# A streaming encoder step on one core: half of the norming, the weights' sums and the GLU's operands move to other places of the program

## The chip, the cores and the metric

The kernel runs on one core of a Trainium2 chip. The core has five engines with queues of their own: TensorE (PE in the profile, PEld for its weight loads), VectorE (DVE), ScalarE (ACT), GpSimd (POOL) and SyncE (SP), which issues the transfers. The metric is the device time of one execution, in microseconds (us). A time given for a kernel is the median of several runs; a profile is one further execution, with a time of its own.

## The reference

One step of a one-layer hybrid encoder over 2048 prompt tokens and 64 tokens of a decode sequence (`D_MODEL` 1024), all in float32. Cut to what matters:

```python
mod = jax.nn.silu(c) @ w_ada + b_ada
shift, scale, gate = jnp.split(mod, 3, axis=-1)
h = _rmsnorm(x, norm_g) * (1.0 + scale[:, None, :]) + shift[:, None, :]
proj = h @ w_in                                   # 1024 x 3080
u, z_s, q, k, v, z_a, f_logit = jnp.split(proj, IN_SPLITS, axis=-1)   # 5 x 512, 512, 8
# S5: 32 groups of 16 channels, 64 complex states each, scan over time
y_ssm = jax.nn.gelu(y_ssm)
y_ssm = y_ssm * jax.nn.sigmoid(y_ssm @ w_glu + b_glu)       # 512 x 512
y_ssm = y_ssm * jax.nn.silu(z_s)
# FoX: 8 heads of 64, q and k normed, logits plus the running sum of log-forget
logf = jax.nn.log_sigmoid(f_logit + b_f)
o = _fox_attend(q, cum_q, pos_q, k, v, cum_k, pos_k)
y_att = o * jax.nn.silu(z_a)
y = x + gate[:, None, :] * (jnp.concatenate([y_ssm, y_att], axis=-1) @ w_out)
```

## The kernel before

A float32 product is made of three products of rounded parts: `mm3` (L145) splits both factors into a high and a low part and issues high by high, low by high and high by low. Each operand of a large product therefore has to be split first: a cast for the high part (L310 on ScalarE, L308 on VectorE) and a subtraction for the low one (L314 on VectorE, L196 on GpSimd).

The stages follow each other on TensorE:

1. **Norm** (class `InProj`). The 16 tiles of 128 prompt tokens and the decode tile form four groups g = 0 to 3. `load` fetches tiles of x (L473 squares, L475 scales them); `norm` turns them by TensorE (L148), applies the adaLN scale and shift (L500, ScalarE) and splits the result h (L308, L314). The scale and shift come from class `Ada`, whose six `chunk`s each read 2 MB of `w_ada` (L402); chunks 4 and 5 make the gate, which is needed only at the end. The parts of h of groups 0 and 2 share one place in SBUF, and so do those of 1 and 3: `put` stores groups 0 and 1 in DRAM, and `get` brings them back.
2. **In-projection**. `line` walks a list of stretches (kind, first column, row, groups, rate, what to do after a group). For each product (24 matmuls: 8 k steps by 3) it issues the product, fetches and splits the next stretch's weights (`fetch`, `part`), evicts the result (`channels` L582 and L572, `natural` L624), and advances a generator `side` by so many steps as the rate says. u of all four groups comes first, since the S5 needs all of it; then k, v, q and z of groups (2, 3); then the same of groups (0, 1).
3. **The side**. What `side` yields step by step is all the work that lies beside the projection: the S5's parameters, its 16 sets of groups (`s5.sets`), its final state, the log-forget sums (`logf`), the attention's `bias`, and `Out.operands`: eight times, four blocks of `w_out` are read, four of their sums are made (L1629, L1631 on VectorE, L196 on GpSimd), split, and stored in DRAM for the Strassen-like output product.
4. **GLU** (class `Glu`), run inside `Attn.glu` together with the maxima of the attention's logits: 16 blocks of 24 matmuls each.
5. **Attention** with the output's weights prepared beside it, and then the **output product**.

The order of the work: TensorE's instructions keep the order in which they are written out while `e.PE.strict` is set, and are otherwise ordered, as on the other engines, by a scheduler that works from a model of the costs; `tc.high_priority()` puts what is inside it ahead, and `tc.keep_in_program_order` pins an instruction. The products use three PSUM banks in turn (`low_132`, `low_136`, `low_140` in the order), the turning of x two others (`low_124`, `low_128`). Every transfer is issued by SyncE in order, so one that waits holds those behind it.

In the kernel before, the first half of u's columns is written out for groups 0 and 1 unstrictly, together with the second half of them; then chunks 4 and 5, the masks, and the norm of groups 2 and 3 are written out, and only then does the strict line begin. The functions, with the line numbers that the profile uses:

## Time and profile before

| what | value |
|---|---|
| median of 3 runs (1470.35 to 1474.24) | 1474.21 us |
| the profiled execution's own time | 1473.12 us |
| its span, first to last instruction | 1471.1 us |
| TensorE busy | 1329.3 us, 90% |
| VectorE busy | 976.3 us, 66% |
| ScalarE, GpSimd busy | 607.5 us, 493.0 us |
| mean granted clock of TensorE | 0.956 |

A row of the timeline reads: start, duration, engine, line, operation, what it writes and reads, and in brackets how long the engine stood idle before it and what ended the idle time. A row of the table by windows reads: the window, its length, then busy time and number of instructions of each engine, the granted clock, the share of the transfer engines and the rate of transfers. Stages can be found in the timeline by TensorE's rows: the projection's products write `low`, those of the GLU write `glu`, the logits write `twin`.

### The profile page before, as it was taken

Reading aid. Unit: us, or ns where it says so; the run is one execution under the profiler, and the core shown is the slowest. Engines: PE = TensorE matmul, PEld = TensorE weight load, DVE = VectorE, ACT = ScalarE, POOL = GpSimd, SP = SyncE. Lnnn points to the kernel's source line nnn. Section 1 sums busy time; section 2 is a strip of 40 time slices with the busy share of each in tenths; the row PEclk is TensorE's granted clock in tenths of the full one; section 3 lists DMA queues with packets and bytes.
Section 4 is the critical chain, followed back from the end, with each engine's and each line's share of the span. In section 5 each row is a group of like instructions: output and inputs, shape, how many; then the busy total and the mean of one; then the engine's idle time right before and its main releaser. Section 6 shows DMA issues by size and latency. Waiting matters only on the chain.

```text
span 1471.1 us, 25856 instructions
## 1 busy us (share of the span) xinstructions
PE 1329.3 (90%) x9160; PEld 1040.8 (71%) x9160; DVE 976.3 (66%) x2404; ACT 607.5 (41%) x1640; POOL 493.0 (34%) x444
## 2 busy tenths in 40 slices
PE   5888999999999799998953989999999999879998
PEld 2874988999889699996843875555555554358887
DVE  2637977787675577553532787788688787346775
ACT  3745134455443354443312434545535545522221
POOL 1101254355222343240122311432423425824443
PEclk9997999999999899999986989999999999989999
DMA  9856323333436534343676852324122111586452
GB/s 341 306 202 178 94 78 92 104 97 95 118 107 203 192 103 128 102 125 113 216 246 200 249 166 56 98 61 138 47 73 66 37 46 44 143 278 221 154 170 86
DMA packets 249474, 204.91 MB, mean 139 GB/s; under 512 B 91296, under 2 KB 217340, under 8 KB 248321
## 3 DMA queue, kind: packets, MB, share of 16 engines
q1 hardware_dynamic: 249344, 203.27, 45.0%
q8 instruction: 72, 1.18, 0.3%
q14 instruction: 58, 0.47, 0.1%
HBM read 137.68 MB, written 65.53 MB: 138 GB/s over the span
## 4 chain that ended last, share of the span: by engine, by line
PE 67%; DVE 10%; DMA 9%; SPq 4%; issue 4%; ACT 3%; POOL 2%; DVEq 0%; ACTq 0%; POOLq 0%
PE low L145 30%; PE bank L145 12%; PE twin L145 12%; PE last L145 9%; DMA x<-in_x_prompt_dram 3%; PE glu L145 3%; DVE pb L1361 2%; PE bank L148 2%; SPq L402 1%; DMA b<-in_w_out_dram 1%; DVE acc L1438 1%; DMA wst<-in_w_in_dram 1%; DMA ost<-in_w_out_dram 1%; SPq L1625 1%; POOL olb L196 1%
## 5 line engine op out<-in xcount | busy, mean ns | idle before, releaser
L145 PE MATMUL low<-whi,h 128*128 128x256 f32 (+1 forms) x1584 | 297.1, 286 | 14.4 <-DVE th L582 10.1
L145 PE MATMUL low<-h,whi 128*128 128x256 f32 (+2 forms) x1152 | 275.4, 331 | 6.2 <-ACT th L572 5.8
L145 PEld LDWEIGHTS low<-whi,h 128*128 128x128 f32 x1584 | 249.4, 191 | 17.0 <-DVE th L582 10.8
L1361 DVE CUSTOM_DVE_ANT_0 pb<-twin,cb 128x512 bf16<-128x512 f32 (+3 forms) x328 | 200.0, 610 | 60.9 <-PE twin L145 51.1
L145 PE MATMUL low<-wlo,h 128*128 128x256 f32 (+1 forms) x816 | 230.2, 285 | 4.8 <-DVE wlo L314 4.7
L145 PEld LDWEIGHTS low<-h,whi 128*128 128x128 f32 x1152 | 197.2, 193 | 24.7 <-ACT th L572 6.8
L345 ACT ACTIVATE p<-twin 128x1024 f32<-128x1024 f32 (+3 forms) x180 | 149.8, 840 | 119.4 <-PE twin L145 110.6
L145 PE MATMUL low<-h,wlo 128*128 128x256 f32 (+2 forms) x576 | 188.9, 329 | 2.2 <-DVE wlo L314 2.2
L145 PEld LDWEIGHTS low<-wlo,h 128*128 128x128 f32 x816 | 155.4, 190 | 7.3 <-DVE wlo L314 6.8
L145 PE MATMUL bank<-p,vt 128*64 128x512 f32 (+3 forms) x704 | 141.5, 524 | 0.0
L145 PE MATMUL twin<-qs,ks 64*128 64x512 f32 (+3 forms) x1056 | 134.0, 359 | 0.0
L145 PEld LDWEIGHTS low<-h,wlo 128*128 128x128 f32 x576 | 111.3, 193 | 11.4 <-DVE wlo L314 2.6
L1438 DVE TENSOR_TENSOR acc<-acc,p 128x1024 f32<-128x1024 f32 (+4 forms) x90 | 90.7, 1008 | 29.2 <-ACT p L345 26.6
L320 POOL TENSOR_TENSOR qss<-qss,mhalf 128x4 f32<-128x4 f32 (+1 forms) x68 | 73.6, 1084 | 102.1 <-DVE qss L319 99.5
L314 DVE TENSOR_TENSOR wlo<-wst,whi 128x512 fp32r<-128x512 f32 (+1 forms) x96 | 68.4, 723 | 53.5 <-ACT whi L310 53.3
L145 PEld LDWEIGHTS twin<-qs,ks 64*128 64x128 f32 x1056 | 94.6, 190 | 11.0
L145 PE MATMUL twin<-sm,kb 64*128 64x512 f32 (+3 forms) x360 | 77.6, 426 | 21.0 <-DVE pm L1361 14.3
L145 PEld LDWEIGHTS bank<-p,vt 128*64 128x64 f32 x704 | 45.1, 140 | 63.8 <-issue 56.0
L310 ACT CAST whi<-wst 128x512 fp32r<-128x512 f32 (+1 forms) x96 | 58.0, 625 | 64.4 <-DMA wst<-in_w_in_dram 48.9
L196 POOL TENSOR_TENSOR x<-x,ot 128x512 f32<-128x512 f32 (+1 forms) x34 | 52.8, 1557 | 88.7 <-DVE ot L1739 70.9
L620 ACT ACTIVATE ev<-low 128x64 f32<-128x64 f32 x256 | 53.6, 224 | 67.7 <-PE low L145 29.2
L145 PEld LDWEIGHTS twin<-sm,kb 64*128 64x128 f32 x360 | 34.3, 186 | 61.1 <-DVE pm L1361 32.7
(434 smaller groups left out, 2621.2 us busy)
## 6 DMA issues: line engine op xcount, KB each, us to landing
wst<-in_w_in_dram SPq DMA_DIRECT2D x48, 512.0 KB
x<-in_x_prompt_dram SPq DMA_DIRECT2D x32, 512.0 KB
h<-h SPq DMA_DIRECT2D x16, 1024.0 KB
wada<-in_w_ada_dram SPq DMA_DIRECT2D x12, 1024.0 KB
cb<-cb_d SPq DMA_DIRECT2D x20, 512.0 KB
out_dram<-ev SPq DMA_DIRECT2D x64, 128.0 KB
out_dram<-x SPq DMA_DIRECT2D x32, 256.0 KB
z_d<-th SPq DMA_DIRECT2D x24, 256.0 KB
```

What stands on the lines that cost most here:

```text
L145: return self.keep(self.pe.matmul(*a, **kw))
L148: return self.keep(self.pe.transpose(*a, **kw))
L196: PL.tensor_tensor(out, x, y, op=op)
L310: i = S.copy(hi, x)
L314: V.tensor_tensor(lo, x, hi, op=ALU.subtract)
L320: PL.tensor_tensor(out, out, bc(mhalf[:out.shape[0]], list(out.shape)), op=ALU.pow)
L345: i = S.activation(out, x, func, **kw)
L402: x = nc.sync.dma_start(w[:, 4 * k2:4 * k2 + 4], e.w_ada[512 * k2:512 * k2 + 512, n * 512:n * 512 + 512] .rearrange("(k p) c -> p k c", p=P))
L620: S.activation(tv[:, h], pv[:, h], AF.Square, accum_out=ss[:r, h:h + 1])
L1361: V.tensor_tensor_reduce(b[:, :n], ps[:, h, :n], cb[:, h, :n], 1.0, NEG, ALU.add, ALU.max, accum_out=self.pm[:, t, h, pi:pi + 1])
L1438: (PL if j else V).tensor_tensor(y[:rows, :, c0:nq], x[:rows, :, c0:nq], p[:rows, :, :n], op=ALU.add)
L1625: e.tc.keep_in_program_order(e.nc.sync.dma_start(b, self.block(i // 2, i % 2, k)[:, ns]))
```

## The change

Seven edits:

1. The **norm of groups 2 and 3** becomes a generator that yields after each pair of k tiles. A new generator `second` loads x of these groups, starts the transfers of adaLN's chunks 4 and 5, scales, norms group 2, finishes the chunks, norms group 3 and starts the S5's setup. It is the first part of the side. The line now begins with u's first product and takes u in four stretches: the first half of the columns for groups 0 and 1, the second half for 0, 1 and 2, the first for 2 and 3, the second for 3.
2. The side's steps are counted in fractions (`share`), so that a rate of 1.5 gives z 12 steps in a stretch where it gave 8 or 10 by whole numbers.
3. Evictions and the splits of the next weights are written inside `high_priority`, the first half of an eviction stands ahead of `after(g)`, the first split comes one product later (`at == 3`), and 256-wide u products are evicted into the ring "ev" with four buffers instead of "th" with two.
4. **Out.operands** is taken one step at a time at every ninth of the S5's sets' steps.
5. **Glu.start** becomes a generator at the end of the side: the transfer of `w_glu` is issued first, its low parts are made on VectorE, one k tile at a step; the first two parts of y are split there too.
6. Six empty steps instead of three after `logf`'s read.
7. In the attention's **last tile** the last two blocks of p are not added up on VectorE; they go as further matmuls into `sums`. Five steps of the output's weights come ahead of the last sums.

The diff, cut to its core:

```diff
@@ InProj.norm
+    def norm(self, g, steps=False):
...
+            if not steps:
+                if (g, i0) not in self.normed:
+                    self.load(g, i0)
+                self.scale(g, i0)
             xs = self.normed.pop((g, i0))
...
                 if s:
                     V.tensor_copy(hi[:, k:k + 2, c0 + w:c0 + 2 * w], lo[:, k:k + 2, c0:c0 + w])
+                yield
@@ InProj.channels
-        x = self.ev.tile([P, 512], F32, tag="th", name="th")
+        if kind == "u" and n == 256:
+            x = self.ev.tile([P, 256], F32, tag="ev", name="ue", bufs=4)
+        else:
+            x = self.ev.tile([P, 512], F32, tag="th", name="th")
@@ InProj.line
-                if nw and at == 2:
-                    self.part(nw)
-                if nw and not cur:
-                    while len(nw.hi) < KT:
+                with self.e.tc.high_priority():
+                    if nw and at == 3:
                         self.part(nw)
+                    if nw and not cur:
+                        while len(nw.hi) < KT:
+                            self.part(nw)
+                    next(b, None)
                 if after and (not cur or cur[1] != g):
                     after(g)
-                next(b, None)
-                for _ in range(int(size * rate)):
+                share += size * (rate[g] if isinstance(rate, dict) else rate)
+                while share >= 1:
+                    share -= 1
                     next(side, None)
-                for _ in b:
-                    pass
+                with self.e.tc.high_priority():
+                    for _ in b:
+                        pass
@@ InProj.logf
-        yield
-        yield
-        yield
+        for _ in range(6):
+            yield
@@ Attn
-        glu.start()
...
-        if acc[j] is None:
+        if tile.last and i >= tile.nb - 2:
+            tile.rest.append((p, rows, c0, n))
+        elif acc[j] is None:
...
+        ops += [(pt[64 * h:64 * h + 64, c0:nq], e.ones[:rows, :64], p[:rows, h, :m])
+                for p, rows, c0, m in tile.rest for h in (1, 0)]
...
+        for _ in range(5):
+            next(weights)
         self.sums(pend[0])
@@ Glu.start
+        st = []
+        for k in range(0, 4, 2):
+            st.append(self.wk.tile([P, 2, SW], F32, tag="wgs", name="wgs"))
+            e.nc.sync.dma_start(st[-1], e.w_glu[P * k:P * k + 256].rearrange("(k p) c -> p k c", p=P))
         for b in range(2):
             self.load(b)
-        for k in range(0, 4, 2):
-            st = self.wk.tile([P, 2, SW], F32, tag="wgs", name="wgs")
-            e.nc.sync.dma_start(st, e.w_glu[P * k:P * k + 256].rearrange("(k p) c -> p k c", p=P))
-            e.split(st, self.wh[:, k:k + 2], self.wl[:, k:k + 2])
+        for _ in range(3):
+            yield
+        for k in range(4):
+            e.split(st[k // 2][:, k % 2], self.wh[:, k], self.wl[:, k], el=e.V, keep=not k)
+            yield
         for b in range(2, 4):
             self.load(b)
         self.gate(0)
         for b in range(2):
             self.part(b)
+            yield
@@ the program
-        ip.line([("u", 0, 0, (0, 1), 0, None), ("u", 256, 256, (0, 1), 0, None)], nothing, w)
-        for n in (4, 5):
-            ad.chunk(n)
         e.masks()
-        for g in (2, 3):
-            ip.norm(g)
...
+        def second():
+            ip.load(2, 0)
+            ip.load(2, 2)
+            yield
+            gates = [ad.steps(n) for n in (4, 5)]
...
+            for n, _ in enumerate(ip.norm(2, True)):
+                if n % 4 == 3:
+                    ip.load(3, n // 4 * 2)
+                yield
+            for x in gates:
+                for _ in x:
+                    pass
+                yield
...
         def rest():
+            yield from second()
             yield from s5_setup
-            yield from s5.sets()
+            ops = (x for i in range(8) for x in out.operands(*divmod(i, 2)))
+            for n, _ in enumerate(s5.sets()):
+                if n % 9 == 6:
+                    next(ops, None)
+                yield
...
             yield from made[0].bias(s5.ps)
-            for i in range(8):
-                yield from out.operands(*divmod(i, 2))
+            made.append(Glu(e))
+            yield from made[1].start()
...
-        ts = [("u", 0, 0, (2, 3), 3, None), ("u", 256, 256, (2, 3), 3, None)]
+        ts = [("u", 0, 0, (0, 1), 0, None), ("u", 256, 256, (0, 1, 2), {0: 1, 1: 2, 2: 2.5}, None),
+              ("u", 0, 0, (2, 3), {2: 2.5, 3: 4}, None), ("u", 256, 256, (3,), 4, None)]
```

How instructions move, at three places. First TensorE where the gate's chunks lie. `wada` are the weights of a chunk, `ms` its copied result, `ident,x` a turned tile of x, `h` the parts of a group (the number after it is the place), `prow` the S5's parameters. Before:

```order
L145 MATMUL low_144<-wada_1_246,cT_0_176 32x512 x4
L148 MATMUL low_128<-ident_0_82,x_0_145 128x64 x2
L148 MATMUL low_124<-ident_0_82,x_0_145 128x64 x2
L145 MATMUL bank_77<-ms_1_257,sel_0_181 32x512
L145 MATMUL bank_81<-ms_1_257,sel_0_181 32x512
L148 MATMUL low_144<-ident_0_82,prow_0_1191 128x32 x4
L145 MATMUL low_140<-h_0_0_307,whi_3_223 128x256
```

The same chunk in the changed kernel:

```order
L145 MATMUL low_136<-h_36864_0_297,whi_2_208 128x256
L145 MATMUL low_136<-h_0_0_296,wlo_2_209 128x256
L145 MATMUL low_144<-wada_0_216,cT_0_165 32x512 x8
L145 MATMUL bank_77<-ms_0_227,sel_0_170 32x512
L145 MATMUL bank_81<-ms_0_227,sel_0_170 32x512
L145 MATMUL low_144<-wada_1_235,cT_0_165 32x512 x8
L145 MATMUL bank_77<-ms_1_246,sel_0_170 32x512
L145 MATMUL bank_81<-ms_1_246,sel_0_170 32x512
L145 MATMUL low_140<-h_0_0_296,whi_4_630 128x256
```

Before, a block of turned tiles of groups 2 and 3, of both chunks and of the parameters stands between two products, with no product inside. Now both chunks stand together between two products of u, with a product of 24 matmuls right ahead and behind; the turned tiles of group 2 stand eight at a time between the products ahead of this place, and those of group 3 between the products after it.

Second, SyncE's transfers of the GLU's weights (`wgs`). `t` are the stored sums of `w_out`, `vt` and `vn` the attention's values, `gz` the gates, `yt` the S5's outputs, `lf` the log-forget values, `z_d<-th` an evicted z product. Before:

```order
L1638 DMA t_69<-pl_3_7573 128x256
L1563 DMA yt_5_8130<-ys_d 128x2x264
L1303 DMA vt_3_9142<-out_dram 128x4x128
L1303 DMA vt_4_9326<-out_dram 128x4x128
L1299 DMA vn_1_9605<-out_dram 64x128
L1550 DMA wgs_0_8047<-in_w_glu_dram 128x2x512
L1569 DMA gz_0_8059<-z_d 128x2x264
L1550 DMA wgs_1_8051<-in_w_glu_dram 128x2x512
```

In the changed kernel:

```order
L1602 DMA gz_0_7884<-z_d 128x2x264
L698 DMA out_dram<-lf_0_118 128x2x64
L699 DMA out_dram<-lf_0_118 8x8x8
L1576 DMA wgs_0_7781<-in_w_glu_dram 128x2x512
L1576 DMA wgs_1_7783<-in_w_glu_dram 128x2x512
L701 DMA lf_0_118<-out_dram 128x16x8
L705 DMA cl_0_7505<-out_dram 64x8
L601 DMA z_d<-th_0_1555 128x2x256
```

The weights' transfers stood behind the last stores of `t` and the attention's values; now they stand between the write and the read of `lf`, in the middle of the last z stretches. The attention's biases and values (`cb` and `vt`) now stand among and behind the last stores of z, ahead of the GLU's third `gz`.

Third, VectorE where the sums of `w_out` are made (`b` are its blocks, `pl` low parts, `w`, `ws`, `btt`, `kd` the S5's). Before:

```order
L582 SCALAR_TENSOR_TENSOR th_0_509<-th_0_509,low_132 128x512
L1629 TENSOR_TENSOR b_143360_0_7515<-b_143360_0_7515,b_141312_0_7513 128x256
L1631 TENSOR_TENSOR t_144384_0_7549<-b_143360_0_7515,b_140288_0_7512 128x256
L314 TENSOR_TENSOR pl_0_7555<-b_143360_0_7515,ph_0_7554 128x256
L314 TENSOR_TENSOR pl_2_7567<-t_144384_0_7549,ph_2_7566 128x256
L582 SCALAR_TENSOR_TENSOR th_1_536<-th_1_536,low_136 128x512
```

In the changed kernel:

```order
L1006 SCALAR_TENSOR_TENSOR kd_0_2756<-ident_0_82,prm_0_1455,low_124 32x16
L1661 TENSOR_TENSOR b_143360_0_2855<-b_143360_0_2855,b_141312_0_2853 128x256
L975 TENSOR_TENSOR btt_0_2747<-btt_0_2747,lin_0_2748 128x256
L1056 TENSOR_TENSOR w_182496_0_2841<-low_128,co_1_2905 128x256
L1057 TENSOR_TENSOR w_184544_0_2842<-pr_0_2805,si_1_2906 128x256
L1058 TENSOR_TENSOR ws_0_2800<-low_128,co_1_2905 128x8
L1059 TENSOR_TENSOR ws_0_2800<-pr_0_2805,si_1_2906 128x8
L1663 TENSOR_TENSOR t_144384_0_3043<-b_143360_0_2855,b_140288_0_2852 128x256
```

A set of sums stood between the evictions of two z products (L582 of the line's last stretches), and an eviction behind it in VectorE's queue waited for the set's blocks. Now it stands among the S5's operations, several hundred instructions earlier.

79 lines of the change are left out of this document (52 added, 27 removed).

## The prediction, made from the trace of the kernel before

> **What bounds the kernel now.** I read the page first, for which engine sets the end, then a table of windows that I cut where TensorE's gaps begin and end, then the waits and the timeline of the windows with much idle time.
>
> ```profile
> PE 1329.3 (90%) x9160; PEld 1040.8 (71%) x9160; DVE 976.3 (66%) x2404; ACT 607.5 (41%) x1640; POOL 493.0 (34%) x444
> PE 67%; DVE 10%; DMA 9%; SPq 4%; issue 4%; ACT 3%; POOL 2%; DVEq 0%; ACTq 0%; POOLq 0%
> ```
>
> TensorE is busy for 90% of the span and holds 67% of the chain of waits. No edit takes a product away, so what can be won is TensorE's idle time, 141.8 us in all. Where it lies stands in the windows (window, its length, then busy us and instructions of PE, PEld, DVE, ACT, POOL, then the granted clock, the share of the transfer engines, GB/s):
>
> ```profile
> 27.00:108.00 81.00, 68.18 (x522) 62.23 (x523) 39.03 (x81) 44.85 (x93) 6.97 (x12) 0.94 0.74 264
> 108.00:137.00 29.00, 21.07 (x91) 8.89 (x90) 19.11 (x45) 17.01 (x37) 3.24 (x8) 0.71 0.74 225
> 137.00:187.00 50.00, 47.77 (x364) 47.16 (x365) 46.23 (x250) 13.72 (x32) 14.75 (x17) 0.97 0.34 90
> 187.00:250.00 63.00, 55.97 (x446) 54.29 (x445) 48.18 (x124) 27.23 (x177) 32.81 (x31) 0.99 0.27 76
> 250.00:450.00 200.00, 196.75 (x1386) 182.86 (x1385) 146.06 (x355) 92.72 (x369) 74.89 (x91) 1.00 0.36 105
> 756.00:792.20 36.20, 0.44 (x2) 0.00 (x1) 7.19 (x14) 4.78 (x10) 5.93 (x9) 0.56 0.94 288
> 792.20:801.40 9.20, 6.84 (x27) 6.23 (x28) 0.00 (x0) 1.95 (x4) 4.66 (x2) 0.50 0.03 10
> 801.40:870.00 68.60, 61.06 (x493) 55.09 (x492) 55.73 (x129) 29.26 (x59) 18.42 (x12) 0.97 0.72 217
> ```
>
> The largest hole is 756 to 792: 36 us with nothing on any compute engine above a fifth, and transfers at 0.94. Second are 27 to 137, with 12.8 and 7.9 us idle. The projection's middle, 250 to 450, has only 3.3.
>
> **The hole ahead of the GLU.** What TensorE waits for between 650 and 870, and what made that late (SyncE, ScalarE and GpSimd in the timeline):
>
> ```profile
> PE glu L145 <- ACT wgh L310: 35.8, 1, 35.8
> PE low L145 <- DMA lf<-out_dram: 5.6, 1, 5.6
> PE glu L145 <- POOL wgl L196: 2.3, 2, 1.7
> ...
> 767.56 1.82 SPq L1625 DMA_DIRECT2D b<-in_w_out_dram  x4
> 785.49 0.53 SPq L1550 DMA_DIRECT2D wgs<-in_w_glu_dram  x1
> ...
> 791.16 1.04 ACT L310 CAST wgh<-wgs 128x1024 fp32r<-128x1024 f32 x1 [16.76 <-DMA wgs<-in_w_glu_dram]
> ...
> 771.63 0.42 DVE L1629 TENSOR_TENSOR b<-b,b 128x256 f32<-128x256 f32 x1 [7.88 <-DMA b<-in_w_out_dram]
> ...
> 762.44 0.59 ACT L345 ACTIVATE th<-low 128x512 f32<-128x512 f32 x1
> ...
> 763.06 0.69 DVE L582 SCALAR_TENSOR_TENSOR th<-th,low 128x512 f32<-128x512 f32 x1
> ```
>
> The GLU's weights are asked for at 785.49, 29 us after the last product, because SyncE first issues the last two sets of w_out's sums, whose stores wait for VectorE, which waits for blocks of w_out behind 0.94 of transfers. The change moves both away: in its order the weights' transfer stands ahead of `lf`'s read, and 8 z products follow the last turning of the attention's bias. The matmul spacing of a z product (0.23 us, below) makes these 8 x 24 x 0.23 = 44 us. The split of w_glu, now four casts and four subtractions of half that width, and of y, fits there beside ScalarE's and VectorE's evictions. The first GLU matmul then waits only for the last eviction to free its PSUM bank: 0.59 + 0.69 us by the rows, with the hand-overs I take 2.5. So 35.8 becomes 2.5: **-33.3** (bounds -34.5 with 1.3 left, and -21 with 14.8 left, for which see below).
>
> **The GLU's start.** Its first matmuls are slow:
>
> ```profile
> 801.18 0.42 PE L145 MATMUL glu<-yh,wgl 128*128 128x264 f32 x1
> 801.40 0.33 PE L145 MATMUL glu<-yh,wgh 128*128 128x264 f32 x1
> 801.57 0.28 PE L145 MATMUL glu<-yl,wgh 128*128 128x264 f32 x1
> 801.69 0.28 PE L145 MATMUL glu<-yh,wgl 128*128 128x264 f32 x1
> ...
> ACT gx L345 <- DMA ms_d<-gx: 8.6, 3, 4.5
> ...
> cb<-cb_d SPq DMA_DIRECT2D x6, 512.0 KB
> vt<-out_dram SPq DMA_DIRECT2D x4, 256.0 KB
> ```
>
> One starts every 0.22 us up to 801.40 and every 0.12 after, and the window 792.2 to 801.4 has a clock of 0.50. Without the hole the clock should stay up: 9.2 - 2.3 of waits = 6.9 us at 0.22 make 31 matmuls, 0.10 us each, 3.1 us; with the 2.3 for `wgl`, **-5.4**. The Trainium skill ("TensorE: Matmul & The Clock Gate", Part 1) puts the slow start at about 3.4 us of busy time; by it this term would be 1.5 us smaller, but the trace shows twice that time, and the trace decides.
>
> Against this stands what the hole hid. `cb` and `vt`, 3 MB and 1 MB, were loaded in it; now a part of them is issued just after the projection's end, since their places hold h until its last product, and the GLU's third `gz` stands behind them in SyncE's queue. 4.25 MB (with one more `vt` from the cache) at the 288 GB/s of the hole are 14.8 us. Half of `cb` can go ahead of the end, 3 transfers, so 2.75 MB or 9.5 us come after, and the first two GLU blocks (2 x 24 x 0.12 = 5.8 us) have their gates by then. ScalarE waited 8.6 us for stores of `ms_d` in this stage already. Bounds 0 and +12; I take **+5**, about 9.5 less 5.8, and something for the stores.
>
> **u's phase.** In the changed order nothing but 8 turnings stands between two products of u, so the 7.9 us of idle time in 108 to 137 go, where TensorE waited at chunks 4 and 5 and behind turnings, and where the clock was 0.71 for 21 busy us. Of 12.8 in 27 to 108 a part stays:
>
> ```profile
> PE low L148 <- ACT hf L500: 4.9, 9, 1.0
> PE bank L145 <- DMA wada<-in_w_ada_dram: 4.4, 2, 3.6
> PE low L148 <- DVE x L475: 4.4, 4, 2.7
> ```
>
> Chunks 0 to 3 and the norm of groups 0 and 1 stand where they stood. Losing chunks 4 and 5 and 4 MB of x from the first 108 us lets the rest land sooner (0.74 and 264 GB/s there). New waits: two of about 1 us for `ms` inside the gate's chunks. And VectorE: 46.2 of 50 us busy in 137 to 187 with the S5's setup, which now starts later, behind norm's 19.1, with fewer products to lie under. I take **-15**: 7.9, 2 of the 137-window, a third of 12.8, 3 for the clock, less 2. Bounds: -23 (all 22.9 idle us) and -3 (the first set of the S5 waits for its setup and gives 12 back).
>
> **The weights' sums.** Grouped by form, 668 to 792:
>
> ```profile
> L314 DVE TENSOR_TENSOR pl<-b,ph 128x256 fp32r<-128x256 f32 x24 | 11.4, 499 | 0.2
> L314 DVE TENSOR_TENSOR pl<-t,ph 128x256 fp32r<-128x256 f32 x8 | 6.5, 818 | 0.0
> L1631 DVE TENSOR_TENSOR t<-b,b 128x256 f32<-128x256 f32 x8 | 3.9, 493 | 0.2
> L1629 DVE TENSOR_TENSOR b<-b,b 128x256 f32<-128x256 f32 x8 | 3.4, 426 | 39.2 <-DMA b<-in_w_out_dram 39.2
> ...
> L196 POOL TENSOR_TENSOR b<-b,b 128x256 f32<-128x256 f32 x8 | 7.6, 946 | 87.2 <-DVE b L1629 87.2
> ```
>
> 25.2 us of VectorE move into the S5's sets. There VectorE was busy for 146 of 200 us; it becomes 171, 86%, and the line's evictions are put ahead, so at 250 to 450 the work fits. Bounds 0 and +8 (one set in three, 3.2 us each, finds no free bank); I take **+3**. The 12 transfers of a set join a stretch where the share is 0.36; four loads hold SyncE 1.82 us, and where a set's single buffers are not free yet, the next stretch's weights (`wst`) wait behind them. With nine steps between two sets that should be rare.
>
> One thing speaks against this place: `pl<-t` takes 818 ns and `pl<-b` 499 for one size, and the slow ones are those beside GpSimd's two operations of a set. The Trainium skill ("SBUF — State Buffer", Who interferes with whom) says that a VectorE instruction with two SBUF inputs contends with a GpSimd one that reads SBUF; the trace agrees. By it the moved sets would meet GpSimd's 37% in this window and cost up to 9 us more of VectorE, still under 200.
>
> **The small ones.** `lf`: three more empty steps, at three steps to a z product of 24 matmuls:
>
> ```profile
> 666.07 0.62 PE L145 MATMUL low<-h,whi 128*128 128x512 f32 x2
> 666.53 0.40 PE L145 MATMUL low<-h,wlo 128*128 128x512 f32 x1
> 672.54 0.77 PE L145 MATMUL low<-lf,triu 128*128 128x128 f32 x2 [5.62 <-DMA lf<-out_dram]
> ...
> 1293.96 1.97 PE L145 MATMUL bank<-acc,ones 128*64 128x512 f32 x4 [3.01 <-DVE acc L1438]
> ```
>
> Two matmuls in 0.46 us, so 5.5 us a product: the three steps cover the 5.62. The 1 MB of `wgs` now ahead of the read can give some back: **-4.6** (0 to -5.6). The evictions first, and splits ahead: 7.0 us idle in 187 to 250 and 3.3 in 250 to 450, of which some are waits for `wlo` and `ev`: **-2** (0 to -5). The last tile: two additions leave the 3.01 us, four matmuls come: **-1.5** (0 to -4).
>
> Sum: -33.3 - 5.4 + 5 - 15 + 3 - 4.6 - 2 - 1.5 = -53.8. The profiled execution took 1473.1, 1.1 under the median, so **1419**.
>
> **Rivals.** (a) *The hole is filled by transfers.* If `gz` and `ms_d` wait out the 14.8 us and 12 us more are lost to stores: +12 on the sum, 1431. For it 0.72 and 217 GB/s in the GLU already; against it, that 23 of 36 us there carried `t` and w_out. (b) *VectorE's backlog behind u.* Norm's 19 and the setup's 46 us press into the last u products, and the first set waits: u gives 3 in place of 15, the sums +8: 1436. (c) *More comes free*: all 22.9 idle us of u, no collision: 1419 - 8 - 5 - 3 = 1403. (d) *The change does not do what it says*: the bias ends late, `w_glu`'s split falls behind the projection, and the 16.8 us for it remain: 1435. In the order 8 products stand behind the bias, which speaks against it. (e) *Slower*: VectorE becomes the bound between 137 and 668.
>
> ```profile
> 137.00:668.00 531.00, 505.21 (x3686) 477.07 (x3686) 378.22 (x1088) 232.81 (x1021) 199.62 (x231) 0.98 0.40 118
> ```
>
> Its 378.2 us with norm's 19.1 and the sums' 25.2 are 422.5 of 531. Each microsecond of GpSimd's 199.6 that held VectorE beyond what these rows already contain would add to that, and past 108.5 the strict line waits for its evictions. To lose the 54 won, and 4.4 more, takes 167 of the 199.6; if all of them did, the time would be 1419 + 91 = 1510. The rows contain the contention of all but the moved work, which speaks against it.
>
> **How the numbers follow.** Forecast 0.55, (a) 0.13, (b) 0.13, (c) 0.11, (d) 0.05, (e) 0.03. The forecast's own bounds are 1408 to 1430; down to (c) less a little and up past (b), 1399 to 1441 leaves about 2 in 10 out. A difference under 0.3%, 4.4 us, can't be told from none. Of (d) and (e) together 0.03 may end within that and 0.03 above, so faster 0.94.
>
> **What would show it.** Right: one gap under 5 us ahead of the first `glu` matmul, released by an eviction; matmuls 0.12 us apart from the first on; the first k product some 15 us before 186.9, with no stretch of turnings alone; `lf` no longer among TensorE's waits. Wrong: waits of `gx` for `ms_d` or of VectorE for `gz` above 15 us in the GLU; TensorE waiting for VectorE's setup after u; VectorE above 95% in the S5's stretch.

## The result: 2.3% faster, two thirds of the forecast gain

The changed kernel takes 1438.32 us (median of 4 runs, 1436.26 to 1441.69), against 1473.69 us for the kernel before in as many runs. The ratio is 0.9767, with a 95% interval of 0.9743 to 0.9791. Its profiled execution took 1438.38 us, with a span of 1436.7. The forecast was 1419; the time lies inside the stated range, 1399 to 1441, but above the forecast's own bounds, 1408 to 1430, where the rivals (a) and (b) stood. So 34.4 us of the span went, where 53.8 had been summed up. The page of the profile after:

```profile
span 1436.7 us, 25846 instructions
PE 1327.0 (92%) x9168; PEld 1041.7 (73%) x9168; DVE 978.9 (68%) x2406; ACT 606.1 (42%) x1642; POOL 494.8 (34%) x442
PE 62%; DVE 14%; DMA 5%; issue 5%; ACT 2%; POOL 2%; SPq 0%; DVEq 0%; ACTq 0%; POOLq 0%
```

TensorE's work is nearly the same, SyncE's 4% of the chain are gone, and VectorE's share of it has grown from 10% to 14%. To see where the time went, I cut both traces at the same six events, read from the starts of TensorE's rows: the first k product (tokens of groups 2 and 3), the first k product of the second half (groups 0 and 1), the last product of the projection, the first `glu` matmul, the first of the attention's `twin<-sm,kb`, and the first `last` product. Stretches in us, of the profiled executions:

| stretch | before | after | difference | forecast |
|---|---|---|---|---|
| start to first k product | 186.9 | 180.5 | -6.4 | -15 |
| to the second half's first k product | 293.8 | 308.6 | +14.8 | +3, and part of -2 |
| to the last product | 275.4 | 272.0 | -3.4 | -4.6, and part of -2 |
| hole ahead of the GLU | 36.2 | 1.8 | -34.4 | -33.3 |
| GLU | 78.1 | 77.0 | -1.1 | -5.4 + 5 |
| attention | 430.1 | 426.5 | -3.6 | -1.5 |
| output product | 170.7 | 170.3 | -0.4 | 0 |

The hole, the GLU and the tail came as summed. Two stretches did not: u's phase gave 6 us in place of 15, and the stretch in which the S5's sets run (the middle stretch below) lost 15. Those two are what the experiments are about. Each stretch is read from one execution; kernels below that leave u's phase alone have 179.5 to 182.3 us for it, and one that leaves the middle stretch alone has 306.4 in place of 308.6, so 2 or 3 us in one stretch are not a finding.

The hole first, in the timeline of TensorE after:

```profile
761.07 0.40 PE L145 MATMUL low<-h,wlo 128*128 128x512 f32 x1
762.88 0.39 PE L145 MATMUL glu<-yh,wgh 128*128 128x264 f32 x1 [1.41 <-DVE th L600]
763.11 0.28 PE L145 MATMUL glu<-yl,wgh 128*128 128x264 f32 x1
763.23 0.28 PE L145 MATMUL glu<-yh,wgl 128*128 128x264 f32 x1
...
777.13 0.59 PE L145 MATMUL glu<-yh,wgh 128*128 128x264 f32 x1 [4.61 <-ACT gx L345]
777.51 0.42 PE L145 MATMUL glu<-yl,wgh 128*128 128x264 f32 x1
777.73 0.42 PE L145 MATMUL glu<-yh,wgl 128*128 128x264 f32 x1
```

35.8 us of waiting became 1.41, released by the last eviction, and from the second matmul on one starts every 0.12 us: the slow start is gone from this place. A part of the gain is given back at 777, as feared: a wait of 4.6 us, behind which the matmuls start 0.22 us apart again, up to 780.15. The chain of waits of that window follows it to a store of the first gated block, issued behind `cb` and `vt`:

```profile
770.75 5.74 DMA ms_d<-gx
...
776.59 0.49 ACT gx L345
```

Now the stretch of the S5's sets, by windows (the columns as in the prediction). After:

```profile
250.00:300.00 50.00, 47.25 (x374) 45.03 (x372) 48.01 (x109) 25.17 (x80) 22.84 (x30) 1.00 0.53 162
300.00:350.00 50.00, 44.43 (x327) 41.77 (x326) 41.19 (x108) 28.99 (x148) 27.20 (x31) 0.93 0.54 165
350.00:450.00 100.00, 92.69 (x558) 82.50 (x557) 80.02 (x177) 43.17 (x157) 39.20 (x45) 0.97 0.50 147
```

Of the 200 us, 15.6 are idle on TensorE, where it was 3.3 before. VectorE is at 96% for the first 50 and at 80 to 82% behind them, and the transfers' share rose from 0.36 to about 0.52. What TensorE waited for over the whole span (us in total, times, longest):

```profile
PE low L145 <- DVE wlo L314: 9.5, 9, 2.2
PE low L145 <- ACT bt L995: 7.5, 6, 4.3
...
PE low L145 <- ACT rot L1101: 5.0, 1, 5.0
...
PE low L145 <- DVE ev L642: 4.6, 4, 1.7
...
PE low L145 <- DMA lf<-out_dram: 2.4, 1, 2.4
```

In the middle stretch alone these are 7.3 us for `bt`, 5.0 for `rot`, 3.4 for `ev` and only 1.3 for `wlo`; most of `wlo`'s 9.5 lies elsewhere. Two of these waits in the timeline:

```profile
209.06 0.56 PE L145 MATMUL low<-whi,h 128*128 128x264 f32 x1 [5.01 <-ACT rot L1101]
...
405.62 2.13 PE L145 MATMUL low<-us,bt 128*128 128x264 f32 x4 [4.32 <-ACT bt L995]
```

At 209 TensorE stands for `rot`, the last piece of the S5's setup: the setup starts later than before, behind the norm (its parameters are turned at 151.5 where it was 136.5). At 405 it stands for `bt`, a constant of a set that ScalarE copies; SyncE's timeline and then the chain of waits show what held the copy:

```profile
396.62 1.84 SPq L1658 DMA_DIRECT2D b<-in_w_out_dram  x4
398.55 0.94 SPq L540 DMA_DIRECT2D wst<-in_w_in_dram  x2
```

```profile
398.55 5.31 DMA wst<-in_w_in_dram
...
403.88 0.02 ACT whi L310
...
404.41 0.40 ACT ph L310
404.81 0.50 ACT th L345
405.30 0.27 ACT bt L995
```

The next stretch's weights (`wst`) are issued behind four blocks of w_out, land 5.3 us later, and their cast `whi` stands on ScalarE, ahead of a split of the sums (`ph`), an eviction (`th`) and then `bt`. Three parts of the change meet in this chain: the sums' transfers, the sums' casts, and the priority of the weights' split. Which of them costs what, the trace alone does not say.

### The profile page after: what moved, and what is told of

The parts are those of the page before. It is cut to its first block, busy times and chain, and to the rows that moved or that the text cites. A ratio compares the mean times of both kernels' runs of the same rounds, so it can differ in the third digit from the quotient of the medians.

```text
span 1436.7 us, 25846 instructions
## 1 busy us (share of the span) xinstructions
PE 1327.0 (92%) x9168; PEld 1041.7 (73%) x9168; DVE 978.9 (68%) x2406; ACT 606.1 (42%) x1642; POOL 494.8 (34%) x442
## 4 chain that ended last, share of the span: by engine, by line
PE 62%; DVE 14%; DMA 5%; issue 5%; ACT 2%; POOL 2%; SPq 0%; DVEq 0%; ACTq 0%; POOLq 0%
PE low L145 24%; PE twin L145 12%; PE bank L145 12%; PE last L145 9%; PE glu L145 2%; DVE pb L1381 2%; PE bank L148 2%; DMA z_d<-th 1%; DMA wst<-in_w_in_dram 1%; DVE acc L1459 1%; DVE wlo L314 1%; POOL olb L196 1%; DMA ms_d<-gx 1%; DMA ost<-in_w_out_dram 1%; DVE pl L314 1%
## 5 line engine op out<-in xcount | busy, mean ns | idle before, releaser
L145 PE MATMUL low<-whi,h 128*128 128x256 f32 (+1 forms) x1584 | 301.3, 288 | 14.1 <-ACT rot L1101 5.0
L145 PEld LDWEIGHTS low<-whi,h 128*128 128x128 f32 x1584 | 252.5, 193 | 17.7 <-ACT rot L1101 5.2
```

What stands on the lines that cost most here:

```text
L145: return self.keep(self.pe.matmul(*a, **kw))
```

## The experiments

Theory A: the sums of w_out among the S5's sets are what the middle stretch lost. Theory B: it is the S5's setup, pushed back by the norm. Theory C: it is the priority. All times below are of the changed kernel with the edit shown, medians of four or five runs, and ratios to the kernel before in the same series, with 95% intervals. The changed kernel itself is 0.9767 (0.9743 to 0.9791); a kernel whose interval overlaps this one is not told apart from it by its time.

### Sums behind the sets

```diff
-            ops = (x for i in range(8) for x in out.operands(*divmod(i, 2)))
-            for n, _ in enumerate(s5.sets()):
-                if n % 9 == 6:
-                    next(ops, None)
-                yield
-            for _ in ops:
-                yield
+            yield from s5.sets()
+            ops = (x for i in range(8) for x in out.operands(*divmod(i, 2)))
+            for _ in ops:
+                for _ in range(3):
+                    yield
...
-                ts.append((kind, base, row, half, {"v": 2, "z": 1.5}.get(kind, 1), after))
+                ts.append((kind, base, row, half, {"v": 2, "z": 1.5 if half[0] else 2.5}.get(kind, 1), after))
```

> The eight sets of w_out's sums are taken behind the S5's last set (three steps between two of them, z of the second half at 2.5 steps to make room), all else as changed. Theory A (the sums among the S5's sets are what made the stretch from the first k product to the first k product of the second half longer, 293.7 us before and 308.6 after): this stretch falls back to about 296, and the time to about 1427. Theory B (the S5's setup, now behind the norm, is what is late there): the stretch stays above 304, and the time within 4 us of 1438.

1428.41 us, ratio 0.9717 (0.9700 to 0.9734): faster than the changed kernel. The middle stretch fell from 308.6 to 287.3 us, shorter than theory A asked for and than the kernel before (293.8). Its window, and then its timeline of what happened later (TensorE, then SyncE and ScalarE):

```profile
180.00:467.00 287.00, 279.96 (x2005) 262.76 (x2003) 220.43 (x596) 127.79 (x567) 112.24 (x131) 0.99 0.38 113
```

```profile
697.65 0.77 PE L145 MATMUL low<-lf,triu 128*128 128x128 f32 x2 [10.04 <-DVE pl L314]
...
752.55 0.59 PE L145 MATMUL glu<-yh,wgh 128*128 128x264 f32 x1 [4.04 <-DVE th L600]
...
684.93 0.40 SPq L698 DMA_DIRECT2D out_dram<-lf  x1
...
691.88 1.84 SPq L1658 DMA_DIRECT2D b<-in_w_out_dram  x4
693.77 0.66 SPq L699 DMA_DIRECT2D out_dram<-lf  x1
694.48 0.44 SPq L701 DMA_DIRECT2D lf<-out_dram  x1
...
751.18 0.60 ACT L345 ACTIVATE th<-low 128x512 f32<-128x512 f32 x1 [7.60 <-DMA z_d<-th]
```

7 us idle where the changed kernel had 22 (309.00 less 287.21 busy, below). So among the S5's sets the sums cost 21 us against this place, 2.7 a set, where I had put +3 for all eight. Not all of it is waiting: nearly the same number of matmuls is busy for 287.2 us there and for 280.0 here, at a granted clock of 0.97 against 0.99, so about 7 us are matmuls that run slower.

Of the 21 us, 11 are left in the span (1436.7 less 1425.3): the second half is 8.9 us longer and the hole 2.6, among smaller differences. The row at 697.65 names VectorE's `pl`, but what was late is the read of `lf`: SyncE writes the two parts of `lf` at 684.93 and 693.77, with the eight stores of a set and the four loads of the next between them, and the read, at 685.09 in the changed kernel, goes out at 694.48. Ahead of the GLU VectorE is idle for 7.5 us; the last eviction waits for ScalarE, and that for the store of an earlier z, which takes 7.6 us to land. So neither wait is the sums' arithmetic. The wait of 5.0 us for `rot` is still there, so theory B is at most a part.

### Sums spread over all the sets

```diff
-                if n % 9 == 6:
+                if n % 18 == 6:
```

> The sets of w_out's sums are taken at every 18th step of the S5's sets instead of every 9th, over all 166 steps instead of the first 80. If it is their density that cost 21 us (VectorE at 96% between 250 and 300), the stretch from the first k product to the first of the second half falls from 308.6 us to about 295, the next one grows by less than 4, and the time is about 1429. If each set costs its 2.7 us wherever it stands among the S5's sets, the loss only moves to the next stretch, and the time stays within 3 us of 1438.

1442.16 us, ratio 0.9803 (0.9770 to 0.9835), a little over what either reading expected. The middle stretch fell to 297.2, as the density reading has it, but the second half rose from 272.0 to 283.0, which it has not. Five of the eight sets are now loaded in the middle stretch (from 253 on, the fifth at 433) and three behind it (483, 552 and 576). The five lose 9.9 us against 287.3, 2.0 each; the three lose 11.0 against the changed kernel's second half, 3.7 each. Of these 11.0, 5.4 are waits for the reload of h, which the changed kernel did not have. The loss moved with the sets, and was no smaller in all.

```profile
180.00:477.00 297.00, 282.52 (x2004) 264.18 (x2003) 234.56 (x623) 132.63 (x585) 122.51 (x141) 0.99 0.44 133
477.00:760.00 283.00, 262.31 (x1687) 236.28 (x1686) 160.85 (x406) 115.80 (x472) 88.08 (x99) 0.97 0.47 145
```

VectorE is at 79% and 57% in these two windows (80% over the changed kernel's middle stretch), and the price is paid all the same. So an average below 100% was no proof that the moved work fits.

### Transfers without the arithmetic

```diff
-        t2 = pre.tile([P, 256], F32, name="t2", bufs=1)
-        e.tc.keep_in_program_order(e.V.tensor_tensor(b22, b22, b12, op=ALU.subtract))
...
-            e.split(x, *hl, el=e.V)
             for i in range(2):
-                e.nc.sync.dma_start(e.t_d[t][k, i][:, ns], hl[i].bitcast(F32))
+                e.nc.sync.dma_start(e.t_d[t][k, i][:, ns], x)
```

> The sums of w_out and their splits are left out: the blocks are loaded as in the changed kernel, and stored as they are, in the same number of transfers. All of VectorE's, ScalarE's and GpSimd's part of the sets is gone, the transfers stay. If VectorE's 29 us are what costs 21 us of TensorE, the stretch is 287 to 292 us and the time about 1420. If it is the transfers (SyncE held, the next weights and z's stores behind them), the stretch stays above 302 and the time above 1432.

This kernel stores the blocks of w_out in place of their sums and leaves out sums and splits; only its time is read. 1432.97 us, ratio 0.9739 (0.9714 to 0.9764). The middle stretch is 299.3: between the two readings. Without the arithmetic 9.3 of the 21.3 us go; 12.0 stay with the transfers alone. Changed kernel first, then this one, with the chain of waits ahead of its longest new wait, 4.5 us for `bt` at 310.79:

```profile
180.00:489.00 309.00, 287.21 (x2009) 268.08 (x2007) 246.26 (x647) 138.10 (x600) 127.74 (x147) 0.97 0.49 148
```

```profile
182.00:482.00 300.00, 284.18 (x2011) 265.58 (x2010) 219.50 (x599) 128.00 (x571) 110.38 (x132) 0.98 0.50 153
```

```profile
302.30 2.70 DMA t<-b
...
305.02 0.33 SPq L1658
...
305.45 3.96 DMA wst<-in_w_in_dram
```

VectorE fell by 27 us to what it was without the sums, and 15.8 us of TensorE's idle time remain, with the share of transfers at 0.50. So by these executions half of the loss or a little more is the 96 transfers of the eight sets (8 x 12), ahead of `wst` and of the S5's own. The rest went with the arithmetic; the arithmetic without the transfers was not run. In the chain SyncE holds the next set's block until a store of the set before has landed, and issues `wst` only behind it. Once issued, `wst` is no slower than elsewhere: it takes about 4 us from issue to cast, with the sums in this stretch or without them. So in this wait it is SyncE's order that costs; for the others that is not shown. One thing differs here: the stored block itself holds the buffer until the store lands, where in the changed kernel the sums and splits hold it. So the 12.0 are not exactly the transfers' share of the 21.3.

### The norm back in one block

```diff
-            yield from second()
...
+        nothing = iter(())
+        ip.line([("u", 0, 0, (0, 1), 0, None), ("u", 256, 256, (0, 1), 0, None)], nothing, w)
+        for n in (4, 5):
+            ad.chunk(n)
         e.masks()
+        for g in (2, 3):
+            for _ in ip.norm(g):
+                pass
...
+        ts = [("u", 0, 0, (2, 3), 3, None), ("u", 256, 256, (2, 3), 3, None)]
```

> u's products, chunks 4 and 5 and the norm of groups 2 and 3 as before the change, all else as changed. Theory A: the norm's new place is worth what the first k product came earlier, 6.35 us, so the time is about 1444. Theory B: the wait of 5.0 us for the S5's setup and part of the other new waits go as well, so the time stays within 3 us of 1438, and the norm's new place is worth nothing.

1448.12 us, ratio 0.9847 (0.9830 to 0.9864), above both expectations. The first k product came at 190.6, 10.1 us later than in the changed kernel, and the middle stretch took 311.5. TensorE's waits from 27 to that product, and the window:

```profile
PE low L148 <- ACT hf L514: 12.0, 14, 2.9
PE low L145 <- DMA wada<-in_w_ada_dram: 7.9, 3, 5.0
```

```profile
27.00:190.60 163.60, 137.46 (x973) 118.89 (x974) 108.98 (x387) 74.47 (x167) 27.27 (x38) 0.87 0.60 198
```

The wait for `rot` is gone here, as theory B had it, and yet the middle stretch is not shorter: there TensorE waits 7.5 us for `ev` (3.4 in the changed kernel), 9.2 for `bt` (7.3) and 5.0 for `wlo` (1.3). Theory B falls as an account of the 15 us. The norm's new place is worth some 10 us beside the other edits. That is more than the 6.4 of the comparison with before, where the same block ended at 186.9: the block is worse off beside the other edits than it was in the kernel before, and which of them does that was not tried.

### The priority taken away, and kept for u alone

```diff
-                with self.e.tc.high_priority():
-                    if nw and at == 3:
-                        self.part(nw)
...
-                    next(b, None)
+                if nw and at == 2:
+                    self.part(nw)
...
+                next(b, None)
```

and `channels` evicts u into the ring "th" again.

> Evictions and the splits of the next weights without priority and at their old places, u evicted into its old ring, all else as changed. Theory A: with VectorE at 96% between 250 and 300 the priority is what keeps TensorE fed; without it the time is 1444 or more. Theory C (the priority puts a cast that waits for weights ahead of what the S5's sets need on ScalarE, as in the wait of 4.3 us at 405): the time falls by 3 to 8 us, to 1430 to 1435.

1448.20 us, ratio 0.9855 (0.9834 to 0.9875). The time is as theory A expected, but not from its place: the first k product comes at 190.0, 9.5 us later, while the middle stretch is 301.8, 6.8 us shorter. Besides, the attention takes 432.2 us where it took 426.5, with none of its lines changed; that is part of the time. The edit helps u's phase and costs in the S5's. So the second kernel keeps the priority for u's stretches only:

```diff
-                with self.e.tc.high_priority():
+                with self.e.tc.high_priority() if kind == "u" else ExitStack():
```

> The priority holds for u's products alone; k, v, q and z are evicted and their weights split without it, all else as changed. With the priority away everywhere, and u's old ring, the first k product came 9.5 us later and the stretch behind it was 6.8 us shorter. If the priority itself costs in that stretch, the first k product stays at 180.5, the stretch is about 302 and the time about 1431. If the shorter stretch was only the later start (the setup's wait of 5.0 us gone), the stretch stays above 306 and the time within 3 us of 1438.

1435.77 us, ratio 0.9769 (0.9737 to 0.9801). In the trace both parts are as expected: the first k product at 181.4, the middle stretch 301.3. The second half starts 6.3 us earlier than in the changed kernel, but 1.5 us are lost behind it and 1.4 in the attention, and the median of the whole can't be told from the changed kernel's. That the priority costs some 5 to 7 us in the middle stretch while the sums are there is what two kernels show; that it is worth leaving out is not shown.

### The GLU's operands

```diff
-            yield from made[1].start()
+            yield
...
+        for _ in glu.start():
+            pass
         self.load()
```

> The GLU's operands are loaded and split behind the projection as before the change, the sums of w_out stay among the S5's sets. If the hole of 35.8 us was mostly the sums and their stores ahead of the GLU's weights, a hole of 10 to 15 us remains and the time is about 1450. If it was the weights' own load and split, the hole is above 25 us and the time above 1462.

1440.76 us, ratio 0.9800 (0.9784 to 0.9817), and no hole: the wait ahead of the first `glu` matmul is 1.5 us. Both expectations miss. The text stands behind the projection, but in the program that is built the transfers stand far ahead of its end:

```profile
682.26 0.89 SPq L1578 DMA_DIRECT2D wgs<-in_w_glu_dram  x2
683.67 0.37 SPq L701 DMA_DIRECT2D lf<-out_dram  x1
```

In the changed kernel they go out at 683.65, from quite another place of the text. So, with the change's other edits in place, taking the sums of w_out away from the end of the side is enough to close the hole; putting the GLU's operands ahead by hand added nothing that this comparison can tell.

### The scaling of group 3 earlier

In u's phase of the changed kernel TensorE still waited, now for the scaled x of group 3, in the strict order:

```profile
118.00 0.48 PE L148 MATMUL low<-ident,x 128*128 128x128 f32 x1 [3.11 <-DVE ss L319]
...
131.80 0.45 PE L148 MATMUL low<-ident,x 128*128 128x128 f32 x1 [2.36 <-ACT sq L484]
133.84 1.75 PE L148 MATMUL low<-ident,x 128*128 128x128 f32 x7 [1.59 <-DVE x L488]
...
116.38 0.15 DVE L319 TENSOR_SCALAR ss<-ss 128x1 f32<-128x1 f32 x1 [3.17 <-ACT sq L484]
```

Square, mean, power and scaling follow each other on ScalarE, VectorE, GpSimd and VectorE, and the turning that needs them is written one or two steps behind. A first try writes all three scalings earlier:

```diff
+            ip.scale(3, 0, True)
             for x in gates:
                 for _ in x:
                     pass
                 yield
-            ip.scale(3, 0, True)
             yield
             for n, _ in enumerate(ip.norm(3, True)):
-                if n == 3:
-                    ip.load(3, 4)
-                    ip.scale(3, 2, True)
-                if n == 6:
-                    ip.scale(3, 4, True)
+                if n == 0:
+                    ip.scale(3, 2, True)
+                    ip.load(3, 4)
+                if n == 4:
+                    ip.scale(3, 4, True)
```

> The scaling of group 3's x is written two to four steps earlier, all else as changed. If TensorE's waits for it in the strict order (1.2, 3.1, 1.0, 2.4 and 1.6 us between 88 and 134) are what was left of u's idle time, the first k product comes at about 173 instead of 180.5, and the time is about 1432. If x lands too late or VectorE's queue is what holds the scaling, the first k product stays after 178 and the time within 3 us of 1438.

1437.25 us, ratio 0.9770 (0.9742 to 0.9798), first k product at 177.5. The decode tile's x is loaded here into the place of the first tile's while most of group 3's turnings of that tile are still to come, so these turn other data, and a wait of 5.4 us for that transfer is part of the time. Together with the spread sums, and with the same flaw:

> Both of these edits. If they are independent their gains add up: about 1423. If the earlier start of the sets only meets the same VectorE, the time is that of the better one alone, about 1429.

1443.01 us, ratio 0.9794 (0.9760 to 0.9829), above both expectations: nothing adds up, first k product at 177.8, middle stretch 297.0, second half 285.1. The third kernel moves two scalings and leaves the load where it was:

```diff
+            ip.scale(3, 0, True)
             for x in gates:
...
-            ip.scale(3, 0, True)
             yield
...
+                if n == 0:
+                    ip.scale(3, 2, True)
                 if n == 3:
                     ip.load(3, 4)
-                    ip.scale(3, 2, True)
```

> Two of group 3's three scalings are written three steps earlier, its loads stay where they are; all else as changed. If TensorE's waits for the scaled x in the strict order (ss, x and sq: 9 us between 88 and 134) are what was left of u's idle time, the first k product comes at 172 to 174 instead of 180.5, and the time is about 1431. If the S5's setup behind it takes the same time to be ready, the 5.0 us wait ahead of the first set grows by what is won, and the time stays within 2 us of 1438.

1435.03 us, ratio 0.9759 (0.9736 to 0.9782), not told apart from the changed kernel. The first k product comes at 176.1, 4.4 us earlier, not the 6.5 to 8.5 expected; the middle stretch is 1.5 longer, and the first set now waits 6.5 us for the setup instead of 5.0. A new wait of 5.3 us for `hf` stands in group 3's norm:

```profile
134.27 0.44 PE L148 MATMUL low<-ident,x 64*128 64x64 f32 x2 [5.26 <-ACT hf L514]
```

So of the 9 us some 4 can be won by writing the scaling earlier, and part of those stays with the setup behind it.

### Sums behind the log-forget sums, and beside them

Both kernels give z of the second half 2.5 steps, as the one with the sums behind the sets did.

```diff
+            for _ in (x for i in range(8) for x in out.operands(*divmod(i, 2))):
+                for _ in range(3):
+                    yield
             made.append(Attn(e))
             yield
             yield from made[0].bias(s5.ps)
```

> The sums of w_out stand behind the log-forget sums and ahead of the attention's bias, three steps between two sets, z of the second half at 2.5 steps; all else as changed. Behind the S5's last set they gave a stretch of 287.3, but held VectorE's queue ahead of the log-forget sums, a wait of 10.0 us. If that wait is all that was lost there, it goes and the time is about 1420. If the sums so close to the end hold the GLU's operands in SyncE's queue again, a hole of 10 us or more opens ahead of the GLU, and the time is above 1430.

1442.05 us, ratio 0.9806 (0.9779 to 0.9832). The middle stretch is 289.1 and the wait of 10 us is gone, since `lf` is read at 658.87, ahead of the first set's loads at 669 (it was SyncE's queue that held it, and not VectorE's as expected), but the hole is back in part:

```profile
757.49 0.59 PE L145 MATMUL glu<-yh,wgh 128*128 128x264 f32 x1 [8.30 <-DVE th L600]
764.43 0.59 PE L145 MATMUL glu<-yh,wgh 128*128 128x264 f32 x1 [5.25 <-ACT yh L310]
```

The last evictions stand behind the sums' splits on VectorE, and the GLU takes 84.1 us instead of 77.0. The GLU's weights go out at 658 and 662 here, so early weights alone do not close the hole while the sums stand late; how much of the 35.8 us they would save is not shown. The last kernel lets the sums run beside the log-forget sums, with the earlier scalings:

```diff
+            for n, _ in enumerate(behind()):
+                if n % 2 == 0:
+                    next(ops, None)
+                yield
+            for _ in ops:
+                for _ in range(2):
+                    yield
```

(`behind` is the S5's final state and `logf`.)

> The sums of w_out behind the S5's last set, but with the log-forget sums running beside them, one set at every second of their steps and the rest two steps apart; with the earlier scalings of group 3, and z of the second half at 2.5 steps. If the gains add up, the first k product comes at 176, the stretch behind it is about 288, the log-forget wait of 10.0 us is gone with a second half of about 274, and the time is about 1418. If the sums' chain of transfers near the end holds the last evictions as behind the log-forget sums (8.7 us ahead of the GLU and 5.3 us inside it), the time is that of the sums behind the last set alone, 1428, or above.

1428.47 us, ratio 0.9707 (0.9690 to 0.9724), the same as the sums behind the sets alone, and both faster than the changed kernel. The stretches are 176.4, 289.7 and 279.8 us, and the hole is 9.1. The wait of 10.0 us has become another:

```profile
673.08 0.69 PE L148 MATMUL low<-ident,cm 128*128 128x128 f32 x2 [7.89 <-DVE cm L723]
755.03 0.59 PE L145 MATMUL glu<-yh,wgh 128*128 128x264 f32 x1 [8.69 <-DVE th L600]
```

The last eviction waits here as in the kernel with the sums behind the sets: VectorE is idle, and the store of an earlier z takes 7.7 us to land. In all three late places a set takes about 11 us, as its single buffers pass through load, sums and stores (loads at 649, 661, 671 and so on in the first), so eight need nearly 90 us. That reaches from the S5's last set to the end of the projection, and something in that stretch waited in each of the three.

## Why the prediction was right, and where it was wrong

- **Why the range held.** The hole is most of the gain, and its term was right. The two terms that missed, u's phase and the weights' sums, missed the same way and put the time 19 us over the forecast. That it stayed inside the range is in part luck: the sums cost 21 us, far over their bound, and the same stretch won some 6 back (287.3 without the sums, against 293.8 before) that the forecast did not have.
- **The hole.** -33.3 forecast, -34.4 measured, with the wait of an eviction in its place, as written. The mechanism was named right in its first half, the sums and their stores ahead of the GLU's weights; its second half, the weights' transfer put ahead by hand, was not needed.
- **The GLU's start.** -5.4 and +5: the matmuls are 0.12 us apart from the second on, where they had been 0.22 for the first 9 us; TensorE's busy time in the stretch fell from 67.9 to 64.1 us and the 2.3 us for `wgl` are gone. Waits for `gx` rose from 2.5 to 6.6 us with `ms_d`'s stores. The sum of both, -0.4, measured -1.1, so both terms were about right. That the clock stays up without the hole was right at the start alone: behind the 4.6 us at 777 it was lowered again. The Trainium skill ("TensorE: Matmul & The Clock Gate", Part 1) has the clock lowered after idle time and raised after some 3.4 us of work. Both traces agree with the first; for the second, the slow matmuls took 3.0 us behind 777, and 9.1 us in the kernel before, with waits of 1.7 and 0.6 us among them.
- **The weights' sums.** The step that failed. "I take +3", with a bound of +8, rested on two things: that VectorE at 86% leaves room, and that the transfers' 0.36 does. It measured 21.3 us against the same kernel with the sums behind the sets: 12.0 with the transfers alone, 9.3 more with the arithmetic. VectorE's load itself came as forecast, 169 of the 200 us where 171 were summed; what failed is the step from there to "the work fits". The bound was too low since it priced only VectorE; the sentence that named `wst` behind the blocks in SyncE's queue had the mechanism of the wait at 310.79 above, but ended with "should be rare", with no number. The Trainium skill ("SBUF — State Buffer", Who interferes with whom) has a VectorE instruction with two SBUF inputs contend with a GpSimd one that reads SBUF. The trace agrees, though the term is small: `pl<-b` took 684 ns in the sets where it was 499,

```profile
L314 DVE TENSOR_TENSOR pl<-b,ph 128x256 fp32r<-128x256 f32 x24 | 16.3, 684 | 0.0
```

  so 4.9 us more of VectorE, within the 9 that were worked out. The 7 that ran beside no GpSimd instruction took 412 ns, the other 17 took 796 on average.
- **u's phase.** -15 forecast, -6.4 measured. In the sum stood the 7.9 us of idle time in 108 to 137, 2 of the window behind it, a third of the 12.8 ahead of it, and 3 for the clock, less 2. The third of 12.8 came (idle time in 27 to 108 fell to 8.0 us, though the row of 4.4 us for `wada` that was shown for it lies before 27), and so did the clock's 3 (busy time fell by 3.6). The 7.9 failed: TensorE's idle time from 27 to the first k product fell only from 23.0 to 20.2 us, and 9 of it again lay between 108 and 137: the block's waits went, and waits for the scaled x of group 3 came. I had named `ms` and the setup as the new waits, and not the four-engine chain of the scaling. Moving it gave 4.4 us.
- **The rivals.** Of (a) only a small part came: TensorE waited 6.6 us for `gx` in the GLU. Of (d) nothing did: the first `glu` matmul waited for an eviction. **Rival (b)** forecast 1436 and came nearest, but not by its mechanism: the setup's backlog on VectorE shows as the 5.0 us for `rot`, and undoing the norm's place did not bring the middle stretch back. **Rival (e)** was right in one thing: VectorE did hold the strict line, but the transfers held it at least as much.
- **The small ones.** `lf`: 5.6 to 2.4 us, so -3.2 of -4.6. The second half lost a wait of 9.3 us for an eviction just behind the reload of h, not forecast, and gave half of it back in waits for `wlo` (0.9 to 5.8 us). The last tile: 3.0 to 1.2, as summed; the attention's -3.6 otherwise lies within what it varies between the kernels here (426.5 to 432.3).
- **The small gain of evictions first** (-2) was a sum of two large terms: some -9.5 in u's phase (with its ring) and +5 to +7 in the S5's stretch while the sums are there.

## What to carry to other kernels

When work moves into a stretch whose busiest engine seems to have room, price each of its transfers in the issuing queue and every engine it passes, and not only the busiest one: here twelve transfers a set cost at least as much as its arithmetic, at an average of half the transfer engines. When a row names what a long wait waited for, look also at the issuing queue: the 10 us put down to VectorE were a read that stood behind other transfers. A hole that a queue makes is closed by moving what stands ahead of it; the waiting work may then move up by itself, as it did here. And where instructions of a chain over several engines are put between strict ones, the chain must start as many products earlier as it is long.

## What was not expected of the hardware

A set of sums cost 2.0 us of TensorE in a stretch where VectorE was at 79% and 3.7 where it was at 57%: the loss does not follow the mean load of that engine. And the transfers alone, at a share of 0.50, made TensorE lose 12 us. In the longest of that kernel's new waits it is SyncE's order; how the rest divides between that order and the transfer engines' load, no run here separates.

Short waits cost more than their length. In the changed kernel, with matmuls 0.12 us apart up to there, one wait of 2.2 us at 581.15 is followed, from 582.2 on, by 3.4 us of matmuls 0.21 us apart; waits of 2.1 to 2.2 us are followed by the same in the kernel with the sums behind the sets (558.94) and in the kernel before (825.06).
